# The end of a one-core block: h read back before the last two experts, their rows finished apart

## The chip, the cores and the metric

One core of a Trainium2 chip runs the whole program. The metric is device time in microseconds for one execution. All times inside an execution are given from the start of its span, the stretch from the first to the last instruction of the program that the profiler recorded. TensorE is called PE, VectorE DVE, ScalarE ACT, GpSimd POOL and SyncE SP.

## What is computed

One layer of a streaming encoder over 1024 tokens of 1024 channels, batch 1: a normalisation and one projection, two mixers (a diagonal state-space model and retention), an output projection that gives h, then a mixture of experts on top of h and a final normalisation. Only the last two matter here:

```python
    h = h + hier_moe(rms_norm(h, norm2_w), ...)
    return rms_norm(h, final_norm_w)

    # hier_moe: each token goes to 2 of 32 experts
    hid = jax.nn.silu(xb @ w_gate[e]) * (xb @ w_up[e])          # 1024 -> 512
    return ((hid @ w_down[e]) * w_b[:, None])                    # 512 -> 1024, added to the token's row
```

`rms_norm` multiplies a row by `rsqrt(mean(x*x) + eps)` and by a weight per channel.

## The kernel before

The sequence is cut into 8 tiles of 128 tokens (`NT = 8`). Mixers and output projection leave h in HBM as `h_d`, and the normalised rows as `hn_d`. A token may be routed to any expert; each expert takes up to 96 tokens (`CAP`), whose indices are a column of `tok` (padded with an index out of bounds) and whose weights are a column of `lacc[:, 1]`. An overflow loop at the very end takes further blocks of an expert that has more; here it runs no pass, but its barrier is executed.

The experts run one after the other, e = 0 to 31. For each, POOL gathers 96 rows of `hn_d` by index (`gather`, three experts ahead), PE transposes them (`x_split`), and every fp32 operand is split into a rounded part `hi` (a cast on ACT, L1241 for weights, L1221 for activations) and the rest `lo` (a subtraction on DVE, L1242 and L1222), so that a product is three matmuls: xh·hi, xh·lo, xl·hi. `in_proj` does gate ("g") and up ("u"), 24 matmuls each (L1267); ACT applies silu (L1378), DVE multiplies (L1387). The hidden rows wait one expert: in iteration e the order of the program is gate of e, then `hid_split` (transposes `ht`, L1275) and `down` of e − 1 (L1287), then up of e. `down` copies its two PSUM halves out with the weights (L1294, tile `yh` or `xy`) and POOL scatters them into `h_d` with an addition (`scatter`, L1210). Each scatter waits for the one before to land.

SP issues all loads of weights, at most six under way, in the order of the list `worder`. Its last four entries are pairs of tiles of h, read back from `h_d` (`wr_load`, L949, tiles `wh_0` to `wh_3`). They are issued once the number of experts scattered reaches `NE - 1`, and wait for the scatter of expert 30.

What follows the last expert: its rows are not scattered. They are gathered from `h_d` into `hg`, and the copy of its sums `y` is added there. Tiles 0 to 5 (`LATE = 6`) are finished without them; into tiles 6 and 7 they are added with a matmul by a selection matrix `late`, which POOL builds in `late_rows` (L1352, L1353). `final` finishes a tile: square with a row sum on ACT (L231), mean plus eps on DVE (L232), power −0.5 on POOL (L233), scaling by factor and channel weight on DVE (L1413); SP stores it (L1416). At the end POOL writes the finished rows `hg` over tiles 0 to 5 by index (L1450), after the stores of those six.

The instructions of each engine run in the order in which they were built. A scheduler makes that order from a simulated timeline; `behind(kind)` tells it to place what follows no earlier than the named instruction. Rows of that order name semaphores: DMAHW those of SP's transfers, DMASW those of POOL's.

Of the kernel before, what the change touches and what calls it, by code (L numbers as in the profile page):

```python
# [13 lines left out]
I32 = mybir.dt.int32  # L14
# [30 lines left out]
VF = 0  # L45
LATE = 6
NX = 3
# [100 lines left out]
def hybrid_block(ctx: ExitStack, tc: tile.TileContext, a: dict, out: bass.AP, dbg=None):  # L148
# [820 lines left out]
    def next_loads(n):  # L969

        while n > 0 and worder and (worder[0][1] != "h" or NDONE[0] >= NE - 1):
            wr_load(*worder.pop(0))
            n -= 1
        return n
# [283 lines left out]
    def in_proj(e, nm, xs):  # L1258
        pt = ps_g.tile([P, 512], F32, tag="g", name=f"{nm}{e}")
        n = 0  # L1260
        for half_ in range(2):
            for c, (hi, lo) in enumerate(take(e, nm, half_)):
                for q in range(2):
                    k = 4 * half_ + 2 * c + q
                    ws = slice(q * 512, q * 512 + 512)
                    for l, r in ((xs[0], hi), (xs[0], lo), (xs[1], hi)):
                        TE.matmul(pt[0:CAP], l[:, k, :], r[:, ws], start=(n == 0), stop=(n == 23))  # L1267
                        n += 1
        return pt
# [77 lines left out]

    def late_rows():

        n = (NT - LATE) * P  # L1350
        sel = late_at[0:CAP]
        G.iota(sel, pattern=[[1, n]], base=LATE * P - OOB, channel_multiplier=0, **small)  # L1352
        G.tensor_scalar(out=sel, in0=sel, scalar1=lacc[:, 0, NE - 1:NE], scalar2=None, op0=ALU.is_equal)  # L1353
        return sel

# [17 lines left out]
    for e in range(NE):  # L1373
# [27 lines left out]
        if e == NE - 2:  # L1401
            tabi, nbk, lasti = made
            late = late_rows()
        prev = (e, hid)


    def final(i, t, n=P):

        junk = yh[:, D + 512:2 * D].bitcast(BF)
        ss = pe.tile([P, 1], F32, tag="ss", bufs=4, name=f"fs{i}")  # L1410
        rr = pe.tile([P, 1], F32, tag="rr", bufs=4, name=f"fr{i}")
        rstd_of(t[0:n], D, ss[0:n], rr[0:n], junk[0:n])
        V.scalar_tensor_tensor(out=t[0:n], in0=t[0:n], scalar=rr[0:n, 0:1], in1=fw[0:n], op0=ALU.mult, op1=ALU.mult)  # L1413

# [4 lines left out]

    hs, last_tok = hid_split(*prev), tok[:, NE - 1:NE]  # L1420
    gather(hg, last_tok, h_d)
    pts = down_mm(NE - 1, hs)
    y = yh[:, 0:D]
    for q in range(2):
        qs = slice(q * 512, (q + 1) * 512)
        at["copy"] = S.activation(y[0:CAP, qs], pts[q][0:CAP], AF.Copy, scale=wts[:, NE - 1:NE])
# [10 lines left out]
    with behind("copy"), behind("split"):
        at["rows"] = V.tensor_tensor(out=hg[0:CAP], in0=hg[0:CAP], in1=y[0:CAP], op=ALU.add)
        for i in range(LATE, NT):
            for q in range(2):  # L1440
                qs = slice(q * 512, (q + 1) * 512)
                pt = (ps_g if q else ps_d).tile([P, 512], F32, tag="g" if q else "d", name=f"la{i}_{q}")
                TE.matmul(pt, late[:, (i - LATE) * P:(i - LATE + 1) * P], y[0:CAP, qs], start=True, stop=True)
                V.tensor_tensor(out=htile(i)[:, qs], in0=pt, in1=htile(i)[:, qs], op=ALU.add)
        for i in range(2, LATE):
            finish(i)
        final("g", hg, CAP)
        for i in range(LATE, NT):
            finish(i)
    rows = G.indirect_dma_start(out=out[0, 0:LATE * P, :], out_offset=bass.IndirectOffsetOnAxis(ap=last_tok, axis=0),  # L1450
                                in_=hg[0:CAP, :], in_offset=None, bounds_check=LATE * P - 1, oob_is_err=False)
    for d in stores[:LATE]:
        tc.add_manual_dep(rows.ins, d.name, SYNC, reason="these rows come after those stored without them")

# [89 lines left out]
```

## Time and profile before

| what | value |
|---|---|
| median of 3 runs | 1106.59 us (1105.11 to 1107.81) |
| the profiled execution, its own time | 1108.12 us |
| its span | 1106.4 us |
| PE busy (matmuls) | 1036.0 us, 94% |
| DVE busy | 851.7 us, 77% |
| ACT busy | 648.7 us, 59% |
| POOL busy | 315.2 us, 28% |
| HBM traffic over the span | 276 GB/s |

Busy time is a union of the instructions' own times. Matmuls are pipelined, so a busy PE is not one at its peak. The experts take the span from about 500 us on; the part that the change touches is the last 60 us. An idle time in brackets behind a row is that of the engine just before it, and the name behind the arrow is what ended it. Transfers show as their issue (SPq, or POOL's DMA_INDIRECT); the time to landing is counted from there.

### The profile page before, as it was taken

To read this page: it belongs to the slowest core of one execution; us is meant where nothing else is said; L and a number is where in the kernel's file an instruction comes from. 1 tells how busy PE (TensorE), PEld (TensorE's weight loads), DVE (VectorE), ACT (ScalarE), POOL (GpSimd) and SP (SyncE) were. 2 spreads that over 40 slices of the span, in tenths; PEclk is the share of its full clock that TensorE was granted. 3 is DMA by queue.
4 is the path that set the end of the run, shared out by engine and by line. 5 is a ranking of instruction groups with operands and counts; after the bars stand their busy time and mean duration, and the time that the engine had idled before them with its cause. 6 is when DMAs were issued, how large, how long until landed. Compare 5 with 4: busy or idle time off the path is not lost. (4 is left out here: it accounts for less than half of the span.)

```text
span 1106.4 us, 15386 instructions
## 1 busy us (share of the span) xinstructions
PE 1036.0 (94%) x5185; PEld 793.2 (72%) x5186; DVE 851.7 (77%) x1221; ACT 648.7 (59%) x867; POOL 315.2 (28%) x402
## 2 busy tenths in 40 slices
PE   6988889999999999988999999999999999999990
PEld 5776777888888888865777777777777777777750
DVE  4785898635446655567998999989898998999874
ACT  6512342243311222236888888888888888888862
POOL 4946477221046521122111010111101010231312
PEclk9988999999999899997999999999999999999995
DMA  8564465563524598867999999999999999999955
GB/s 307 214 190 101 89 190 130 147 207 114 181 77 153 197 341 275 286 267 258 358 362 384 365 380 374 363 352 353 371 349 373 359 360 356 387 359 365 384 172 209
DMA packets 88132, 305.88 MB, mean 276 GB/s; under 512 B 14588, under 2 KB 35324, under 8 KB 63472
## 3 DMA queue, kind: packets, MB, share of 16 engines
q1 hardware_dynamic: 80160, 287.38, 71.9%
q0 software_dynamic: 7280, 17.01, 6.4%
q8 instruction: 42, 0.69, 0.3%
q10 hardware_dynamic: 608, 0.46, 0.1%
q14 instruction: 42, 0.34, 0.1%
HBM read 266.05 MB, written 39.85 MB: 276 GB/s over the span
## 5 line engine op out<-in xcount | busy, mean ns | idle before, releaser
L1242 DVE TENSOR_TENSOR wlou<-wu,whiu 128x1024 fp32r<-128x1024 f32 x128 | 156.0, 1224 | 35.1 <-ACT whiu L1241 23.5
L1242 DVE TENSOR_TENSOR wlod<-wd,whid 128x1024 fp32r<-128x1024 f32 x128 | 153.8, 1216 | 3.4 <-PE dn L1287 1.2
L1242 DVE TENSOR_TENSOR wlog<-wg,whig 128x1024 fp32r<-128x1024 f32 x127 | 151.2, 1218 | 2.5 <-ACT whig L1241 0.2
L1241 ACT CAST whiu<-wu 128x1024 fp32r<-128x1024 f32 x128 | 134.2, 1048 | 25.3 <-PE dn L1287 16.7
L1241 ACT CAST whig<-wg 128x1024 fp32r<-128x1024 f32 x127 | 130.7, 1052 | 29.2 <-PE u L1267 28.3
L1241 ACT CAST whid<-wd 128x1024 fp32r<-128x1024 f32 x128 | 134.2, 1049 | 23.2 <-PE g L1267 14.2
L1267 PE MATMUL g<-wlog,xh 128*96 128x512 f32 x254 | 102.1, 402 | 0.0
L1267 PE MATMUL u<-whiu,xl 128*96 128x512 f32 x256 | 101.5, 396 | 0.0
L1267 PE MATMUL u<-whiu,xh 128*96 128x512 f32 x256 | 101.1, 395 | 0.0
L1267 PE MATMUL g<-whig,xh 128*96 128x512 f32 x254 | 100.8, 397 | 0.0
L1267 PE MATMUL g<-whig,xl 128*96 128x512 f32 x254 | 100.5, 396 | 0.0
L1267 PE MATMUL u<-wlou,xh 128*96 128x512 f32 x256 | 100.2, 391 | 0.0
L1287 PE MATMUL dn<-wlod,xh 128*96 128x512 f32 x256 | 99.6, 396 | 0.0
L1287 PE MATMUL dn<-whid,xl 128*96 128x512 f32 x256 | 96.1, 396 | 0.0
L1210 POOL DMA_INDIRECT h_d<-xy,tok x16 | 28.2, 1761 | 212.6 <-ACT xy L1294 196.7
L1287 PE MATMUL dn<-whid,xh 128*96 128x512 f32 x256 | 87.5, 395 | 0.6 <-ACT xh L1221 0.6
L1210 POOL DMA_INDIRECT h_d<-yh,tok x15 | 22.8, 1522 | 179.4 <-ACT yh L1294 163.3
L1287 PEld LDWEIGHTS dn<-whid,xh 128*96 128x96 f32 x256 | 41.6, 162 | 18.8 <-ACT xh L1221 0.8
L1267 PEld LDWEIGHTS u<-wlou,xh 128*96 128x96 f32 x256 | 41.4, 162 | 18.2
L1287 PEld LDWEIGHTS dn<-whid,xl 128*96 128x96 f32 x256 | 41.6, 163 | 17.8
L1267 PEld LDWEIGHTS u<-whiu,xl 128*96 128x96 f32 x256 | 41.1, 161 | 18.1
L1267 PEld LDWEIGHTS u<-whiu,xh 128*96 128x96 f32 x256 | 41.3, 161 | 17.8
(396 smaller groups left out, 2332.5 us busy)
## 6 DMA issues: line engine op xcount, KB each, us to landing
wg<-in_moe_w_gate_dram SPq DMA_DIRECT2D x64, 1024.0 KB
wu<-in_moe_w_up_dram SPq DMA_DIRECT2D x64, 1024.0 KB
wd<-in_moe_w_down_dram SPq DMA_DIRECT2D x64, 1024.0 KB
wr<-in_w_in_dram SPq DMA_DIRECT2D x19, 512.0 KB
xt<-in_x_dram SPq DMA_DIRECT2D x8, 512.0 KB
woraw<-in_w_out_dram SPq DMA_DIRECT2D x8, 512.0 KB
h<-in_x_dram SPq DMA_DIRECT2D x8, 512.0 KB
h_d<-h SPq DMA_DIRECT2D x8, 512.0 KB
```

Of the source, the lines that this page charges most:

```text
L1210: return G.indirect_dma_start(out=h_d, out_offset=bass.IndirectOffsetOnAxis(ap=idx, axis=0), in_=y[0:CAP, :], in_offset=None, bounds_check ...
L1241: S.copy(hi, raw)
L1242: at["split"] = V.tensor_tensor(out=lo, in0=raw, in1=hi.bitcast(F32), op=ALU.subtract)
L1267: TE.matmul(pt[0:CAP], l[:, k, :], r[:, ws], start=(n == 0), stop=(n == 23))
L1287: TE.matmul(pts[q][0:CAP], l[:, k, :], r[:, ws], start=(k == 0 and n == 0), stop=(k == 3 and n == 2))
```

## The change

`APART = 2` takes the place of `LATE = 6`. The four loads of h may be issued after 30 experts, and no longer see experts 30 and 31. All eight tiles are finished and stored without these two experts' rows. The rows of both are finished apart: expert 31's in `hg` as before, expert 30's gathered into `hg2` after its scatter. A token that both experts have would be written twice; `spread` and `only` compare the two lists (one small transpose on PE, four small DVE operations) and move such tokens out of bounds in `tokx`, the list for `hg2`. Two indexed writes end the program, each over all 1024 rows, after all eight stores.

The factors are made for two tiles at a time: `square` on ACT puts row sums (already divided by 1024, through the scale of the activation) into columns of `msqf`, `factors` adds eps (DVE, for the first pair POOL) and takes the power on POOL for two columns at once, `scaled` multiplies. The last expert's sums go from PSUM into `hg` with one DVE operation per half (weight and addition), squared per half. The selection matrix, its matmuls and `late_rows` are gone.

```diff
-LATE = 6
+APART = 2
-        while n > 0 and worder and (worder[0][1] != "h" or NDONE[0] >= NE - 1):
+        while n > 0 and worder and (worder[0][1] != "h" or NDONE[0] >= NE - APART):
...
-    def down_mm(e, hs):
+    def down_mm(e, hs, between=None):
         pts = [ps_d.tile([P, 512], F32, tag="d", name=f"dn{e}_{q}") for q in range(2)]
         for half_ in range(2):
-            for c, (hi, lo) in enumerate(take(e, "d", half_)):
+            with behind("square") if half_ else nullcontext():
+                pieces = take(e, "d", half_)
+            if between and not half_:
+                hs = between()
+            for c, (hi, lo) in enumerate(pieces):
...
-    def late_rows():
...
+    def spread():
+        V.tensor_copy(late_at[0:CAP, 0:CAP], lacc[:, 0, NE - 1:NE].to_broadcast([CAP, CAP]))
+
+    def only():
+        pt = ps_t.tile([P, 512], F32, tag="t", name="tx")
+        TE.matmul(pt[0:CAP, 0:CAP], late_at[0:CAP, 0:CAP], ident[0:CAP, 0:CAP], start=True, stop=True)
+        same, both = late_at[0:CAP, P:P + CAP], late_at[0:CAP, P + CAP:P + CAP + 1]
+        V.tensor_scalar(out=same, in0=pt[0:CAP, 0:CAP], scalar1=lacc[:, 0, NE - 2:NE - 1], scalar2=None, op0=ALU.is_equal)
+        V.tensor_reduce(out=both, in_=same, axis=AX.X, op=ALU.max)
+        V.tensor_scalar(out=both, in0=both, scalar1=float(OOB), scalar2=lacc[:, 0, NE - 2:NE - 1], op0=ALU.mult, op1=ALU.add)
+        V.tensor_scalar(out=tokx, in0=both, scalar1=float(OOB), scalar2=None, op0=ALU.add)
...
+        if e == NE - 1:
+            with behind("proj"), behind("cut"):
+                only()
         if prev is not None:
             hs = hid_split(*prev)
             down(prev[0], hs)
...
-            late = late_rows()
+            with behind("cut"):
+                spread()
...
+    def first_tiles():
+
+        with behind("whi"):
+            square(htile(0), 0)
+            square(htile(1), 1)
+        with behind("scatter"):
+            factors(0, 2, eng=G)
+        with behind("factors"):
+            gather(hg, last_tok, h_d)
+            at["factors"] = gather(hg2, tok[:, NE - 2:NE - 1], h_d)
+        with behind("split"):
+            finish(0)
+        with behind("square"):
+            hs = hid_split(*prev)
+        with behind("cut"):
+            finish(1)
+        return hs
+
+    pts = down_mm(NE - 1, None, first_tiles)
+    with behind("cast"):
+        square(htile(2), 2)
+        square(htile(3), 3)
+    with behind("square"), behind("split"), behind("factors"):
+        factors(2, 4)
+        for i in (2, 3):
             finish(i)
...
+        for i in range(4, NT):
+            square(htile(i), i)
+            if i % 2:
+                factors(i - 1, i + 1)
+                for j in (i - 1, i):
+                    finish(j)
+    with behind("square"), behind("factors"):
+        square(hg2[0:CAP], NT)
+        factors(NT, NT + 1, CAP)
+
+    with behind("split"):
+        for q in range(2):
+            qs = slice(q * 512, (q + 1) * 512)
+            V.scalar_tensor_tensor(out=hg[0:CAP, qs], in0=pts[q][0:CAP], scalar=wts[:, NE - 1:NE], in1=hg[0:CAP, qs],
+                                   op0=ALU.mult, op1=ALU.add)
+            square(hg[0:CAP, qs], NT + 1 + q)
...
+    scaled(hg2[0:CAP], fac[0:CAP, NT:NT + 1])
+    scaled(hg[0:CAP], fac[0:CAP, NT + 1:NT + 2])
+
+    def rows_out(t, idx):
+        rows = G.indirect_dma_start(out=out[0], out_offset=bass.IndirectOffsetOnAxis(ap=idx, axis=0),
+                                    in_=t[0:CAP, :], in_offset=None, bounds_check=T - 1, oob_is_err=False)
+        for d in stores:
+            tc.add_manual_dep(rows.ins, d.name, SYNC, reason="these rows come after those stored without them")
+
+    with behind("factors"):
+        rows_out(hg2, tokx[:, 0:1])
+        rows_out(hg, last_tok)
```

Three places show what the built order makes of this. The first is iteration 31, where the gate of expert 31 ends and the down product of expert 30 begins. On ACT `xh<-ht` is the cast of expert 30's transposed hidden rows, `yh<-g` is silu, `whid` and `whiu` are the rounded parts of down and up weights. Before:

```order
L1241 CAST whid_01_9825<-wd_0_9363 128x1024
L1221 CAST xh<-ht_9812 128x384
L1241 CAST whid_10_9841<-wd_1_9391 128x1024
L1378 ACTIVATE yh<-g_9770 96x512
L1241 CAST whid_11_9845<-wd_1_9391 128x1024
L1241 CAST whiu_00_9867<-wu_0_9413 128x1024
```

In the change:

```order
L1241 CAST whid_01_9839<-wd_0_9364 128x1024
L1241 CAST whid_10_9855<-wd_1_9392 128x1024
L1388 ACTIVATE yh<-g_9778 96x512
L1241 CAST whid_11_9859<-wd_1_9392 128x1024
L1221 CAST xh<-ht_9826 128x384
L1241 CAST whiu_00_9881<-wu_0_9414 128x1024
```

On PE, in the same place, the transposes `ht` and the gate's last products; before:

```order
L1267 MATMUL g_9770<-whig_01_9775,xl 96x512
L1267 MATMUL g_9770<-whig_10_9791,xh 96x512
L1275 MATMUL ht_9812<-cst_g,yh 128x96 x4
L1267 MATMUL g_9770<-wlog_10_9792,xh 96x512
L1267 MATMUL g_9770<-whig_10_9791,xl 96x512
L1267 MATMUL g_9770<-whig_10_9791,xh 96x512
```

In the change (`tx` is the small transpose of `only`):

```order
L1267 MATMUL g_9778<-wlog_11_9804,xh 96x512
L1267 MATMUL g_9778<-whig_11_9803,xl 96x512
L1359 MATMUL tx<-cst_g,ovf 96x96
L1275 MATMUL ht_9826<-cst_g,yh 128x96 x4
L1291 MATMUL dn_0_9833<-whid_00_9835,xh 96x512
L1291 MATMUL dn_0_9833<-wlod_00_9836,xh 96x512
```

The transposes moved from inside the gate product behind its end, and their cast moved behind silu and behind the second half of the down weights.

The second place is POOL's queue from the scatters of experts 27 to 30 on (`h_d<-yh`, `h_d<-xy`). Before:

```order
L1352 IOTA ovf 96x256 [waits DVE_49,PE_49]
L1353 TENSOR_SCALAR ovf<-ovf,lacc 96x256 [waits Pool_49]
L1210 DMA h_d<-yh,tok 1024x1024 [waits DMASW1_49,Activation_49]
L1210 DMA h_d<-xy,tok 1024x1024 [waits DMASW3_49,Activation_49]
L1210 DMA h_d<-yh,tok 1024x1024 [waits DMASW4_49,Activation_49]
L1210 DMA h_d<-xy,tok 1024x1024 [waits DMASW6_49,DMASW5_49,Activation_49]
L1205 DMA fwh<-h_d,tok 96x1024 [waits DMASW6_49]
L233 TENSOR_TENSOR fr_9971<-fs_9970,half_c 128x1 [waits DVE_49]
```

In the change, from the scatter of expert 28 to the end:

```order
L1210 DMA h_d<-xy,tok 1024x1024 [waits DMASW3_49,Activation_49]
L1210 DMA h_d<-yh,tok 1024x1024 [waits DMASW4_49,Activation_49]
L1210 DMA h_d<-xy,tok 1024x1024 [waits DMAHW5_49,DMAHW0_49,DMAHW6_49,DMASW6_49,DMAHW7_49,DMASW5_49,Activation_49]
L1442 TENSOR_SCALAR msqf<-msqf 128x2 [waits Activation_49]
L1443 TENSOR_TENSOR msqf<-msqf,half_c 128x2 [waits Pool_49]
L1205 DMA fwh<-h_d,tok 96x1024 [waits DMASW6_49]
L1205 DMA ovf<-h_d,tok 96x1024 [waits DMASW0_49,DVE_49]
L1443 TENSOR_TENSOR msqf<-msqf,half_c 128x2 [waits DVE_49] x3
L1443 TENSOR_TENSOR msqf<-msqf,half_c 96x1 [waits DVE_49]
L1503 TENSOR_TENSOR msqf<-msqf,half_c 96x1 [waits DVE_49]
L1508 DMA out_dram<-ovf,tokx 1024x1024 [waits DMAHW4_49,DMAHW3_49,DMAHW5_49,DMAHW2_49,DMAHW6_49,DMAHW1_49,DMAHW7_49,DMAHW0_49,DVE_49]
L1508 DMA out_dram<-fwh,tok 1024x1024 [waits DMASW2_49,DMASW1_49,DVE_49]
```

Before, POOL's queue ended so:

```order
L233 TENSOR_TENSOR fr_10019<-fs_10018,half_c 128x1 [waits DVE_49,Pool_49]
L233 TENSOR_TENSOR frg<-fsg,half_c 96x1 [waits DVE_49,Pool_49]
L233 TENSOR_TENSOR fr_10032<-fs_10031,half_c 128x1 [waits DVE_49,Pool_49]
L233 TENSOR_TENSOR fr_10039<-fs_10038,half_c 128x1 [waits DVE_49,Pool_49]
L1450 DMA out_dram<-fwh,tok 768x1024 [waits DMAHW4_49,DMAHW3_49,DMAHW5_49,DMAHW2_49,DMAHW6_49,DMAHW1_49,DMASW0_49]
```

The two selections left the head of the scatters; the scatter of expert 30 now names four DMAHW semaphores, those of the loads of h; gathers stand between the factors of the first pair and those of the second; the one indexed write behind six stores became two, the first behind eight, the second with two DMASW semaphores.

The third place is the tail on ACT and DVE behind the last up product. ACT before:

```order
L1241 CAST whid_01_9932<-wd_0_9481 128x1024
L1241 CAST whid_10_9948<-wd_1_9513 128x1024
L1241 CAST whid_11_9952<-wd_1_9513 128x1024
L1221 CAST xh<-ht_9916 128x384
L231 ACTIVATE yh,fs_9970<-wh_0_9875 128x1024
L231 ACTIVATE yh,fs_9977<-wh_0_9875 128x1024
L1426 ACTIVATE yh<-dn_0_9926,lacc 96x512
L1426 ACTIVATE yh<-dn_1_9927,lacc 96x512
L231 ACTIVATE yh,fs_9997<-wh_1_9877 128x1024
```

In the change:

```order
L1241 CAST whid_01_9929<-wd_0_9482 128x1024
L1439 ACTIVATE yh,msqf<-wh_0_9722 128x1024 x2
L1221 CAST xh<-ht_9945 128x384
L1241 CAST whid_10_9966<-wd_1_9514 128x1024
L1241 CAST whid_11_9970<-wd_1_9514 128x1024
L1439 ACTIVATE yh,msqf<-wh_1_9724 128x1024 x2
L1439 ACTIVATE yh,msqf<-wh_2_9726 128x1024 x2
L1439 ACTIVATE yh,msqf<-wh_3_9728 128x1024 x2
L1439 ACTIVATE yh,msqf<-ovf 96x1024
```

DVE before (`wlod` the down weights' rest, `yh<-u` the hidden product, `wh` tiles of h):

```order
L1242 TENSOR_TENSOR wlod_00_9929<-wd_0_9481,whid_00_9928 128x1024
L1242 TENSOR_TENSOR wlod_01_9933<-wd_0_9481,whid_01_9932 128x1024
L1242 TENSOR_TENSOR wlod_10_9949<-wd_1_9513,whid_10_9948 128x1024
L1387 TENSOR_TENSOR yh<-u_9866,yh 96x512
L1222 TENSOR_TENSOR xl<-ht_9916,xh 128x384
L1242 TENSOR_TENSOR wlod_11_9953<-wd_1_9513,whid_11_9952 128x1024
L232 TENSOR_SCALAR fs_9970<-fs_9970 128x1
L232 TENSOR_SCALAR fs_9977<-fs_9977 128x1
L1413 SCALAR_TENSOR_TENSOR wh_0_9875<-wh_0_9875,fr_9971,fwh 128x1024
```

In the change:

```order
L1242 TENSOR_TENSOR wlod_00_9926<-wd_0_9482,whid_00_9925 128x1024
L1242 TENSOR_TENSOR wlod_01_9930<-wd_0_9482,whid_01_9929 128x1024
L1400 TENSOR_TENSOR yh<-u_9880,yh 96x512
L1222 TENSOR_TENSOR xl<-ht_9945,xh 128x384
L1242 TENSOR_TENSOR wlod_10_9967<-wd_1_9514,whid_10_9966 128x1024
L1242 TENSOR_TENSOR wlod_11_9971<-wd_1_9514,whid_11_9970 128x1024
L1442 TENSOR_SCALAR msqf<-msqf 128x2
L1430 SCALAR_TENSOR_TENSOR wh_0_9722<-wh_0_9722,msqf,fwh 128x1024 x2
L1442 TENSOR_SCALAR msqf<-msqf 128x2
L1430 SCALAR_TENSOR_TENSOR wh_1_9724<-wh_1_9724,msqf,fwh 128x1024 x2
L1442 TENSOR_SCALAR msqf<-msqf 128x2
L1430 SCALAR_TENSOR_TENSOR wh_2_9726<-wh_2_9726,msqf,fwh 128x1024 x2
```

On ACT two squares moved ahead of the last hidden cast and all the others follow each other behind the weights; on DVE the third piece of the down weights moved behind the hidden product, and the scalings follow each other in pairs.

## Rows read from the trace of the kernel before

**Rows 1.** The page's span; queue instructions of L1540 (count, ns min/median/max, starts)

```profile
span 1106.4 us, 15386 instructions
...
L1540 POOLq DRAIN  x3: 46/108/5385, 1100.1 to 1106.1; - x3
```

**Rows 2.** Timeline of POOL: start us, us, line, what, [idle before <-releaser]

```profile
1022.73 0.35 POOL L1352 IOTA ovf<- 96x256 f32 x1 [22.59 <-PE tbm L1338]
...
1024.49 1.78 POOL L1210 DMA_INDIRECT h_d<-yh,tok  x1 [0.18 <-issue]
...
1047.74 1.86 POOL L1210 DMA_INDIRECT h_d<-yh,tok  x1 [9.12 <-DMA h_d<-xy,tok]
1062.42 1.42 POOL L1210 DMA_INDIRECT h_d<-xy,tok  x1 [12.82 <-ACT xy L1294]
1068.57 1.03 POOL L1205 DMA_INDIRECT fwh<-h_d,tok  x1 [4.73 <-DMA h_d<-xy,tok]
...
1076.12 1.53 POOL L233 TENSOR_TENSOR fr<-fs,half_c 128x1 f32<-128x1 f32 x1 [0.60 <-DVE fs L232]
...
1094.64 0.98 POOL L1450 DMA_INDIRECT out_dram<-fwh,tok  x1 [1.99 <-DMA out_dram<-wh]
```

**Rows 3.** DMA issues of 1066 to 1107; last number: us to landing

```profile
fwh<-h_d,tok POOLq DMA_INDIRECT x1, 8.1
out_dram<-fwh,tok POOLq DMA_INDIRECT x1, 4.7
```

**Rows 4.** SP's stores to the output in 1090 to 1092

```profile
L1416 SPq DMA_DIRECT2D out_dram<-wh x1: 332/332/332, 1090.5 to 1090.5; - x1
```

**Rows 5.** Timeline of DVE, the last 40 us

```profile
1067.67 0.68 DVE L1387 TENSOR_TENSOR yh<-u,yh 96x512 f32<-96x512 f32 x1
...
1082.97 1.29 DVE L1444 TENSOR_TENSOR wh<-la,wh 128x512 f32<-128x512 f32 x2 [2.81 <-DMA wh<-h_d]
...
1092.18 2.48 DVE L1413 SCALAR_TENSOR_TENSOR wh<-wh,fr,fwh 128x1024 f32<-128x1024 f32 x2 [0.38 <-POOL fr L233]
```

**Rows 6.** Waits of SP's queue, 1030 to 1107: us, times, longest

```profile
SPq L949 <- DMA h_d<-xy,tok: 22.3, 1, 22.3
```

**Rows 7.** Timeline of SP's queue

```profile
1068.36 2.25 SPq L949 DMA_DIRECT2D wh<-h_d  x4
```

**Rows 8.** Timeline of ACT

```profile
1008.36 1.26 ACT L1294 ACTIVATE yh<-dn,lacc 96x512 f32<-96x512 f32 x2
...
1043.73 1.25 ACT L1294 ACTIVATE yh<-dn,lacc 96x512 f32<-96x512 f32 x2
...
1055.58 0.59 ACT L1378 ACTIVATE yh<-g 96x512 f32<-96x512 f32 x1 [0.34 <-PE g L1267]
1056.07 1.04 ACT L1241 CAST whid<-wd 128x1024 fp32r<-128x1024 f32 x1
...
1068.99 0.48 ACT L1221 CAST xh<-ht 128x384 fp32r<-128x384 f32 x1 [1.25 <-PE ht L1275]
1073.51 1.06 ACT L231 ACTIVATE yh<-wh 128x1024 bf16<-128x1024 f32 x1 [4.05 <-DMA wh<-h_d]
...
1074.70 1.06 ACT L231 ACTIVATE yh<-wh 128x1024 bf16<-128x1024 f32 x1
```

**Rows 9.** Timeline of PE, expert 31

```profile
1052.49 0.49 PE L1275 MATMUL ht<-cst_g,yh 96*128 96x96 f32 x4
...
1055.15 0.39 PE L1267 MATMUL g<-whig,xl 128*96 128x512 f32 x1
1055.38 0.62 PE L1287 MATMUL dn<-whid,xh 128*96 128x512 f32 x2
...
1066.26 0.40 PE L1267 MATMUL u<-whiu,xl 128*96 128x512 f32 x1
```

**Rows 10.** The four scatters from 1000 on (L1210)

```profile
DMA to landing us min/median/max: 5.9/9.5/12.4
```

**Rows 11.** Windows: us, busy us of each engine, PEclk, DMA share, GB/s

```profile
1069.90:1073.30 3.40, 3.40 (x10) 2.20 (x9) 1.38 (x2) 0.00 (x0) 0.00 (x0) 0.50 0.94 367
```

More of the change, by code (lines that the diff above doesn't have):

```diff
@@ L1240, in w_split @@
         hi, lo = pair or [pe.tile([P, 1024], F32R, tag="w" + c, bufs=NHL[c], name=f"w{c}{nm}") for c in ("hi", "lo")]
-        S.copy(hi, raw)
+        at["whi"] = S.copy(hi, raw)
         at["split"] = V.tensor_tensor(out=lo, in0=raw, in1=hi.bitcast(F32), op=ALU.subtract)
@@ L1266, in in_proj @@
                     for l, r in ((xs[0], hi), (xs[0], lo), (xs[1], hi)):
-                        TE.matmul(pt[0:CAP], l[:, k, :], r[:, ws], start=(n == 0), stop=(n == 23))
+                        at["proj"] = TE.matmul(pt[0:CAP], l[:, k, :], r[:, ws], start=(n == 0), stop=(n == 23))
                         n += 1
@@ L1346, in tables @@
         yield tabi, nbk, lasti
-    def late_rows():
[L1350 to L1354, printed above, removed]
+    tokx = pl_.tile([CAP, 1], I32, name="tokx")
+    def spread():
[8 more added lines that the diff above has]
+        V.tensor_scalar(out=tokx, in0=both, scalar1=float(OOB), scalar2=None, op0=ALU.add)
     first = [gather(xg[e], tok[:, e:e + 1]).ins for e in range(NX)]
@@ L1392, in hybrid_block @@
             fw, hg = fwh[:, 0:D], fwh[:, D:2 * D]
-            late_at = ovf[:, 2048 - (NT - LATE) * P:2048]
+            late_at = ovf[:, 2048 - 2 * P:2048]
             nc.sync.dma_start(fw, a['final_norm_w'].to_broadcast([P, D]))
@@ L1409, in final, with scaled, square, factors @@
         junk = yh[:, D + 512:2 * D].bitcast(BF)
-        ss = pe.tile([P, 1], F32, tag="ss", bufs=4, name=f"fs{i}")
-        rr = pe.tile([P, 1], F32, tag="rr", bufs=4, name=f"fr{i}")
+        ss = pe.tile([P, 1], F32, tag="ss", bufs=2, name=f"fs{i}")
+        rr = pe.tile([P, 1], F32, tag="rr", bufs=2, name=f"fr{i}")
         rstd_of(t[0:n], D, ss[0:n], rr[0:n], junk[0:n])
-        V.scalar_tensor_tensor(out=t[0:n], in0=t[0:n], scalar=rr[0:n, 0:1], in1=fw[0:n], op0=ALU.mult, op1=ALU.mult)
+        scaled(t[0:n], rr[0:n, 0:1])
+    def scaled(t, r):
+        at["scaled"] = V.scalar_tensor_tensor(out=t, in0=t, scalar=r, in1=fw[0:t.shape[0]], op0=ALU.mult, op1=ALU.mult)
+    msqf = pe.tile([P, 2, NT + 3], F32, name="msqf")
+    msq, fac = msqf[:, 0], msqf[:, 1]
+    def square(t, j):
+        n, f = t.shape
+        junk = yh[:, D + 512:D + 512 + f // 2].bitcast(BF)
+        at["square"] = S.activation(junk[0:n], t, AF.Square, scale=1.0 / math.sqrt(D), accum_out=msq[0:n, j:j + 1])
+    def factors(j0, j1, n=P, eng=V):
+        eng.tensor_scalar(out=msq[0:n, j0:j1], in0=msq[0:n, j0:j1], scalar1=EPS, scalar2=None, op0=ALU.add)
+        at["factors"] = G.tensor_tensor(out=fac[0:n, j0:j1], in0=msq[0:n, j0:j1],
+                                        in1=half_c[0:n, 0:1].to_broadcast([n, j1 - j0]), op=ALU.pow)
     def store(i, t):
         return nc.sync.dma_start(out[0, i * P:(i + 1) * P, :], t).ins
[L1420 to L1426, printed above, removed]
+    last_tok, hg2 = tok[:, NE - 1:NE], ovf[:, 0:D]
     htile = lambda i: wq[(NE, "h", i // 2)][:, (i % 2) * 1024:(i % 2) * 1024 + 1024]
@@ L1430, in finish @@
     def finish(i):
-        final(i, htile(i))
+        scaled(htile(i), fac[:, i:i + 1])
         stores.append(store(i, htile(i)))
-    with behind("cast"), behind("split"):
-        for i in range(2):
-            finish(i)
[L1437 to L1453, printed above, removed]
+    def first_tiles():
[14 more added lines that the diff above has]
+        return hs
@@ new lines, in hybrid_block @@
+    with behind("split"):
[4 more added lines that the diff above has]
+            square(hg[0:CAP, qs], NT + 1 + q)
+    last_sq = msq[0:CAP, NT + 1:NT + 2]
+    V.scalar_tensor_tensor(out=last_sq, in0=last_sq, scalar=EPS, in1=msq[0:CAP, NT + 2:NT + 3], op0=ALU.add, op1=ALU.add)
+    at["factors"] = G.tensor_tensor(out=fac[0:CAP, NT + 1:NT + 2], in0=last_sq, in1=half_c[0:CAP, 0:1], op=ALU.pow)
```

## The prediction, on record before the result

> **What bounds the kernel now.** I read the trace from its end. The span closes at 1106.4 us. The last long entry is a drain of POOL of 5.4 us that begins at 1100.1, in the barrier around the overflow loop, which runs no pass here [rows 1]. Ahead of that barrier stands one transfer: the indexed write of the last expert's rows (L1450). POOL starts it at 1094.64 [rows 2] and it lands 4.7 us later [rows 3], at 1099.3. So the span ends 7.1 us after the last indexed write has landed, and this distance is the same in both programs.
>
> What starts that write? Its row says that POOL stood idle until a store of `out_dram` landed [rows 2]. It is the store of tile 5, which SP issued at 1090.5 [rows 4], so 4.1 us pass from the store that matters to the start of the write. The stores follow DVE, which scales the last pair of tiles from 1092.18 to 1094.66 [rows 5]. Why is DVE that late? The reading of h waited: SP stood 22.3 us for the scatter of expert 30 [rows 6] and issued the four loads from 1068.36 on [rows 7]. ACT's first square waited 4.05 us for the first of them, until 1073.51 [rows 8], and DVE 2.81 us for the last, until 1082.97 [rows 5]. The tail is one string: scatter 30, h, squares, scaling, stores, indexed write, barrier. Ahead of it PE sets the pace, one matmul of 512 columns each 0.23 us without a hole [rows 9].
>
> **The change, part by part.**
>
> 1. *h is read two experts early.* The loads now wait for scatter 29. In this trace POOL started it at 1047.74 [rows 2]; the last four scatters took 5.9 to 12.4 us to land, median 9.5 [rows 10], so about 1057.3. It will come sooner: the two instructions that selected the late rows (L1352, L1353) are gone from POOL's queue. The first stood there waiting for PE until 1022.73, so that scatter 27 went at 1024.49 [rows 2], though its copy on ACT was done by 1009.6 [rows 8]; scatter 29 in turn sat 9.12 us until scatter 28 had landed [rows 2], though its copy ended at 1045.0 [rows 8]. With the chain unblocked I let 29 start at 1045.3 and land at 1054.8. The four loads then run alone. Before, the first landed 5.1 us after its issue and the last 14.6 us after it [rows 5, 7, 8], beside a gather and two stores. Alone I estimate 12.6, so the last of h is there at 1067.4; at worst, with 1057.3 and 14.6, at 1071.9.
>
> 2. *What stands behind it on POOL.* Scatter 30 now waits for all four loads (the DMAHW names in its row). It starts at 1067.6 and, with the queues idle, takes the 5.9 us of [rows 10]: 1073.5. Behind it in POOL's queue stand the factors of tiles 0 and 1, which need no landing, then two gathers that need scatter 30, then the factors of tiles 2 and 3. Two gathers of 1.03 us [rows 2] and their start end at 1075.9; a power took up to 1.53 us on POOL [rows 2], so 1077.4. DVE wants those factors at 1077.7 (below). The cover is 0.3 us, and past it every microsecond counts in full. The first gather, started at 1073.8, lands at 1081.9 if it takes the 8.1 us of [rows 3] again; DVE adds its rows after tile 5, at 1082.7.
>
> 3. *A hole on PE in expert 31.* `only()` is placed behind the gate's last matmul, and the built order has expert 30's transposes (`ht`) there too; they stood inside the gate product before. On ACT their cast `xh<-ht` now follows silu and the cast of `whid_11`. Before, the last gate matmul started at 1055.15 and the first down matmul at 1055.38; the transposes inside cost 0.28 [rows 9]. Now the gate ends 0.28 sooner, silu starts 0.43 later as before, so at 1055.30, the next cast 0.49 behind it and lasts 1.04 [rows 8], the cast of ht takes 0.48 more: PE resumes at about 1057.3. The hole is 1.9 us. The few small DVE operations of `spread` and `only` lie inside it.
> What reaches the tail is less. Before, the product of up and silu (L1387) started 1.41 us after the last up matmul began, at 1066.26 [rows 5, 9], because DVE was still splitting three pieces of the down weights; now the third stands behind it. I take 0.5 us in place of 1.4, so 1.0 of the 1.9 stays; the bounds are 0 and 1.9. The last hidden cast moves from 1068.99 [rows 8] to 1070.0. The squares of tiles 0 and 1, now ahead of it on ACT, have their h since 1060 and fit into ACT's idle time there.
>
> 4. *The tail on ACT and DVE.* From 1070.0: cast 0.5, two casts of weights 1.0 each, two squares (2 and 3) 1.2 each, as the two squares of [rows 8] stand apart: 1074.9. On DVE the step "add eps" for tiles 2 and 3 stands ahead of the scaling of tile 0, so DVE starts at 1075.1. It scales eight tiles at 1.24 each (2.48 for a pair [rows 5]), 9.9 us, with two sums of 96 rows between (1.3 us, as the pair at L1444 [rows 5]) and 0.3 for small steps: 1086.6, against 1094.66 before. This is the gain, 8.1 us. The products with the selection matrix, their four additions and the copy of the last expert's sums are gone; DVE's share of that is in the difference.
>
> 5. *Two lists in place of one, one behind the other.* Before, the write waited for six stores, and the last two landed beside it. Now the first list waits for all eight, and the second for the landing of the first (its row in POOL's order names two software queues). So 4.1 us from the last store to the first list: 1090.7. Its price: 4.7 measured with two stores beside it [rows 3]; without them less, but not below the 0.98 of issue [rows 2] plus the transfer. I take 4.6 for each: 1095.3, 0.2 to start the second, 1100.1. Before, 1099.3. The scaling of the two sets of rows (2.5 us on DVE behind 1086.6) is hidden behind the last store's landing.
> The sum has 9.2 us for the two lists. The Trainium skill ("DMA: Bandwidth & Descriptors", section "Anatomy of one DMA — SWDGE (gpsimd) path") has about 2.0 us fixed plus bytes at 436 GB/s, mostly spent on confirming the write; by it 0.39 MB would be an estimated 2.9 us, 3.9 with the issue measured here, and the sum 1.4 us lower. It also speaks against the change: that fixed cost is now paid twice in a row.
>
> **The sum.** 1100.1 plus 7.1 is 1107.2 in the span, 0.8 above 1106.4. DVE's last scaling of a tile comes 8.1 sooner, but the way from there to the end of the span grows from 11.7 to 20.6 us: it now waits for the last store, not the sixth, and for a second list. The profiled execution took 1108.12, 1.7 over its span and 1.5 over the median of 1106.59; it would be 1108.9. For the median I forecast 1106.59 + 0.8 = 1107.4.
>
> **The rivals.**
> *Slower, POOL's queue:* scatter 29 lands at 1057.3 as before and the loads take 14.6 as before. Scatter 30 starts at 1071.9 and lands at 1077.8, the gathers are out at 1080.2, the factors at 1081, 3.4 us after DVE wants them: 1110.8. It decides from a landing of scatter 30 later than 1073.8. For it: landings from 5.9 to 12.4, and a cover of 0.3. Against it: from 1068 on nothing else moves, and scatter 30 had its 5.9 in such a quiet. A smaller share of it would be seen within the forecast.
> *Slower, the clock:* after the idle at 1066.7 the granted clock stood at 0.50 for the 3.4 us from 1069.9 [rows 11]; PE did ten matmuls in place of some fifteen. If the new hole does the same, PE loses another 1.5: 1108.9, at the edge of what can be told.
> *Faster, cheap lists:* the lists and the last store run with nothing beside them, 4.0 for each list and 0.8 off the 4.1 (estimates: the rows show both with company), and DVE takes up the whole hole (1.0): 1107.4 − 1.2 − 0.8 − 1.0 = 1104.4. For it: the bound of 0 in step 3. Against it: three terms must all come out low.
> *Faster, the change does not do what its order says:* the second list does not stay for the first, and 4.8 us go: 1102.6.
>
> **How the numbers follow.** Forecast 0.57; POOL's queue 0.20; clock 0.08; cheap lists 0.10; no second wait 0.05. About 0.2%, 2.2 us, is what a measurement here tells from no change, so "same" is 1104.4 to 1108.8. Slower: POOL's queue, half of the clock and a little of the forecast's own upper end, 0.27. Faster: no second wait, most of the cheap lists, 0.13. Same: 0.60. The range takes in the forecast, the clock and most of POOL's queue, and below it the cheap lists: 1104.2 to 1110.2.
>
> **What the profile of the changed kernel would show.** The loads of h issued near 1055 (right) or 1057 and later (the slower rival). A hole on PE near 1055 with `xh<-ht` on ACT behind it. Scatter 30 issued when the last h lands, near 1067.6. DVE's scalings from 1075 to 1086.6 without a wait for POOL. Two indexed writes, the second started just after the first landed, and 7.1 us from the last landing to the end. I am wrong if DVE's last scaling ends much off 1086.6, or if the time from it to the end is not some 20.6 us.

## The result, and the profile after

The changed kernel takes 1113.13 us (median of 20 runs, 1109.32 to 1116.73); the kernel before took 1107.53 in the same sessions. The ratio is 1.0051, with a 95% interval of 1.0039 to 1.0063: about 5.6 us slower. I had forecast 1107.4, and a range that ended at 1110.2.

Its profiled execution took 1116.12 us, with a span of 1114.4. Part of the distance to the 1106.4 of before [rows 1] lies ahead of anything that the change touches. One and the same matmul of the first expert, in PE's timeline of before:

```profile
514.38 0.39 PE L1267 MATMUL u<-whiu,xl 128*96 128x512 f32 x1
```

and of after:

```profile
518.54 0.40 PE L1267 MATMUL u<-whiu,xl 128*96 128x512 f32 x1
```

A window ahead of it (us, busy us of PE, weight loads, DVE, ACT and POOL with their counts, granted clock, DMA share, GB/s), before:

```profile
350.00:394.00 44.00, 41.09 (x270) 35.88 (x269) 29.94 (x51) 12.03 (x17) 28.95 (x33) 0.92 0.62 209
```

and after:

```profile
350.00:394.00 44.00, 40.23 (x250) 36.03 (x249) 29.27 (x50) 10.87 (x15) 27.79 (x26) 0.84 0.54 183
```

Up to that matmul the same code took 4.2 us longer; in this window of it the mean granted clock of TensorE was 0.84 in place of 0.92. So I count every profile from that matmul to the end of its span, and call that length its tail. Both kernels were profiled twice more for that (below, h1 and h2):

| kernel | ratio to before, interval | first expert at | span | tail: from there to the end |
|---|---|---|---|---|
| before | 1 | 514.4; 511.7; 514.4 | 1106.4; 1102.8; 1105.6 | 592.0; 591.1; 591.2 |
| after | 1.0051 (1.0039 to 1.0063) | 518.5; 512.0; 513.4 | 1114.4; 1106.5; 1109.1 | 595.9; 594.5; 595.7 |
| e1, lists side by side | 1.0008 (0.9992 to 1.0024) | 515.3 | 1110.0 | 594.7 |
| e2, a weight load less | 1.0014 (1.0001 to 1.0027) | 517.4 | 1111.4 | 594.0 |
| e3, scatter 30 elsewhere | 0.9995 (0.9981 to 1.0009) | 514.5 | 1106.1 | 591.6 |
| e4, no hole on PE | 1.0057 (1.0041 to 1.0073) | 518.1 | 1112.6 | 594.5 |
| g1, gathers last | 1.0050 (1.0032 to 1.0069) | 516.1 | 1116.4 | 600.3 |
| f1, neither wait | 0.9986 (0.9971 to 1.0000) | 515.6 | 1106.2 | 590.7 |
| f3, f1 with a new tail | 0.9958 (0.9942 to 0.9974) | 514.2 | 1102.7 | 588.5 |

From the first expert on the change costs 3.9 us (mean 595.37 against 591.43). Up to the copy of expert 29's sums the two run level: it starts at 1047.83, in the kernel before at 1043.73 [rows 8], 4.1 us apart as the first expert is. What follows is the end of the span, in the times of the profile shown; to set them beside the prediction's, take 4.2 off.

The loads of h are issued behind scatter 29, as planned. The timeline of SP's queue:

```profile
1046.88 2.82 SPq L952 DMA_DIRECT2D wd<-in_moe_w_down_dram  x2
1058.31 3.13 SPq L949 DMA_DIRECT2D wh<-h_d  x4
```

and its waits (us, times, longest):

```profile
SPq L949 <- DMA h_d<-yh,tok: 8.6, 1, 8.6
```

1058.3 is 1054.1 on the clock of the prediction, which had 1054.8. The wait is 8.6 in place of 22.3 [rows 6]. But the loads don't run alone. Windows from their issue on:

```profile
1058.30:1062.00 3.70, 2.21 (x14) 1.60 (x13) 3.02 (x5) 2.61 (x4) 0.00 (x0) 1.00 0.81 298
1062.00:1066.00 4.00, 4.00 (x19) 2.75 (x18) 3.16 (x5) 2.38 (x3) 0.00 (x0) 1.00 1.02 420
1066.00:1070.00 4.00, 4.00 (x19) 2.81 (x18) 3.12 (x3) 3.92 (x6) 0.00 (x0) 1.00 1.03 411
1070.00:1074.00 4.00, 3.18 (x16) 1.91 (x14) 3.08 (x4) 1.56 (x2) 0.00 (x0) 1.00 0.28 105
1074.00:1077.20 3.20, 1.06 (x3) 0.74 (x4) 0.69 (x2) 3.17 (x7) 0.00 (x0) 0.89 0.05 17
```

The next-to-last column is the reading: all sixteen DMA engines are busy from 1062 to 1070 (0.81 of them before that), then a few, and from 1074 to 1077.2 a share of 0.05, less than one engine of sixteen. The trace's landing records say the same of the fourth load: eleven of its sixteen parts land by 1070.95, two near 1071.9, two near 1074.5, the last at 1077.11. The last part of expert 31's last weight load had landed only at 1066.03, 7.7 us after the first load of h was issued. From there the last parts of the four loads follow at 1068.58, 1071.11, 1073.63 and 1077.11.

The records don't name the DMA engine, but the distance from the last part of the weights to the last part of h is nearly the same in all seven profiles in which scatter 30 waits for h: 11.1 us in the three of the changed kernel, in e1 and in e2, 11.0 in g1, 10.8 in e4. What differs is how late the weights end, 5.5 to 8.8 us after the first load of h was issued, and with it the whole reading of h takes 16.3 to 19.9. Before, where the weights had ended 5.8 to 7.2 us ahead of the first load of h, all sixteen parts of a load landed within 1.4 us of each other.

What stands behind the last part is POOL. Its queue's waits ahead of scatter 30, by line (ns min, median, max; first and last start):

```profile
L1210 POOLq EVENT_SEMAPHORE  x3: 43/43/8527, 1068.6 to 1077.3; - x3
```

and its timeline, with the copy on ACT that scatter 30 takes:

```profile
1066.68 1.25 ACT L1298 ACTIVATE xy<-dn,lacc 96x512 f32<-96x512 f32 x2
...
1078.02 1.57 POOL L1210 DMA_INDIRECT h_d<-xy,tok  x1 [27.24 <-ACT whid L1241]
...
1079.98 0.74 POOL L1443 TENSOR_TENSOR msqf<-msqf,half_c 128x2 f32<-128x2 f32 x1
1083.91 1.09 POOL L1205 DMA_INDIRECT fwh<-h_d,tok  x1 [3.19 <-DMA h_d<-xy,tok]
1085.31 0.99 POOL L1205 DMA_INDIRECT ovf<-h_d,tok  x1 [0.30 <-issue]
1086.33 1.39 POOL L1443 TENSOR_TENSOR msqf<-msqf,half_c 128x2 f32<-128x2 f32 x2
...
1099.32 0.97 POOL L1508 DMA_INDIRECT out_dram<-ovf,tokx  x1 [2.38 <-SPq L1521]
1103.37 0.92 POOL L1508 DMA_INDIRECT out_dram<-fwh,tok  x1 [3.08 <-issue]
```

Scatter 30 had its copy at 1068 and went at 1078.0. (The releaser named in its bracket, ACT, had long been done; the semaphore row above shows the true wait.) The gathers stayed for its landing, the factors of tiles 2 to 5 for the gathers, and DVE for the factors. DVE's timeline:

```profile
1080.76 2.48 DVE L1430 SCALAR_TENSOR_TENSOR wh<-wh,msqf,fwh 128x1024 f32<-128x1024 f32 x2 [0.35 <-POOL msqf L1443]
...
1087.08 2.48 DVE L1430 SCALAR_TENSOR_TENSOR wh<-wh,msqf,fwh 128x1024 f32<-128x1024 f32 x2 [3.76 <-POOL msqf L1443]
...
1093.26 2.47 DVE L1430 SCALAR_TENSOR_TENSOR wh<-wh,msqf,fwh 128x1024 f32<-128x1024 f32 x2
```

The tiles end at 1095.73, which is 1091.6 by the clock of before: 3.1 us sooner than there [rows 5], not 8.1. Then come the two lists in a row, and the barrier (POOL's drain, ns and first start, as in [rows 1]):

```profile
L1602 POOLq DRAIN  x3: 46/108/5548, 1108.0 to 1114.1; - x3
```

### The profile page after: what moved, and what is told of

Its sections match the earlier page's. It is cut to its first block, busy times and chain, and to the rows that moved or that the text cites. A ratio compares the mean times of both kernels' runs of the same rounds, so it can differ in the third digit from the quotient of the medians.

```text
span 1114.4 us, 15369 instructions
## 1 busy us (share of the span) xinstructions
PE 1036.3 (93%) x5179; PEld 796.1 (71%) x5180; DVE 851.4 (76%) x1220; ACT 648.8 (58%) x869; POOL 309.1 (28%) x400
## 5 line engine op out<-in xcount | busy, mean ns | idle before, releaser
L1210 POOL DMA_INDIRECT h_d<-xy,tok x16 | 25.9, 1617 | 234.9 <-ACT xy L1298 200.1
L1210 POOL DMA_INDIRECT h_d<-yh,tok x15 | 22.2, 1477 | 196.0 <-ACT yh L1298 189.0
## 6 DMA issues: line engine op xcount, KB each, us to landing
wr<-in_w_in_dram SPq DMA_DIRECT2D x19, 512.0 KB, 7.5
xt<-in_x_dram SPq DMA_DIRECT2D x8, 512.0 KB, 6.5
woraw<-in_w_out_dram SPq DMA_DIRECT2D x8, 512.0 KB
h<-in_x_dram SPq DMA_DIRECT2D x8, 512.0 KB
h_d<-h SPq DMA_DIRECT2D x8, 512.0 KB, 4.3
```

The lines of the kernel that those rows point to most:

```text
L1210: return G.indirect_dma_start(out=h_d, out_offset=bass.IndirectOffsetOnAxis(ap=idx, axis=0), in_=y[0:CAP, :], in_offset=None, bounds_check ...
```

## The experiments

All edits are to the changed kernel unless said. Lengths "to the end" are those of the table.

**e1, the lists side by side.**

```
+        return rows.ins
...
-        rows_out(hg2, tokx[:, 0:1])
-        rows_out(hg, last_tok)
+        apart = rows_out(hg2, tokx[:, 0:1])
+        tc.declare_no_dep(rows_out(hg, last_tok), apart, reason="no row stands in both lists")
...
```

> The second list no longer stays for the landing of the first (no row stands in both). Theory (the two lists in a row cost their full price): the second starts about 1.0 us after the first, as soon as POOL has issued it, in place of 4.05, so 3.0 to 3.5 us go from the end: the time stands at 1.0020 to 1.0025 of before in place of 1.0051, some 2.3 us above it. Rival (the software queue moves one list after the other anyway): the second still lands 3.5 us behind the first, and the time stays at 1.005.

POOL's timeline:

```profile
1097.00 0.97 POOL L1508 DMA_INDIRECT out_dram<-ovf,tokx  x1 [2.38 <-SPq L1522]
1098.28 0.93 POOL L1508 DMA_INDIRECT out_dram<-fwh,tok  x1 [0.30 <-POOLq L1522]
```

and the lists' time to landing (last number, us):

```profile
out_dram<-ovf,tokx POOLq DMA_INDIRECT x1, 3.1
out_dram<-fwh,tok POOLq DMA_INDIRECT x1, 4.4
```

The second list starts 1.28 us behind the first in place of 4.05, and takes 4.4 in place of some 3.6 beside it. From the first list to the end of the span it is 13.0 us, against 15.1: 2.1 us. The tail of the table is only 0.7 shorter, since in this execution the way to the first list was longer than in the changed kernel (581.7 us from the first expert, against 579.6 to 580.8). The runs give 4.7, from two ratios that are each uncertain by more than 1 us. I had expected 3.0 to 3.5: the profile shows less and the runs more. So the second list's place in a row costs 2 us by the profile, up to 4.7 by the runs, and the rival, which had the time stay at 1.005, falls.

**e2, one weight load less.**

```
-    worder += [(NE - 1, "d", 0), (NE - 1, "d", 1)]
+    worder += [(NE - 1, "d", 0)]
...
-        t = wq[(e, nm, half_)]
+        t = wq[(e, nm, 0 if (e, nm) == (NE - 1, "d") else half_)]
```

> The last of expert 31's eight weight loads (1 MB of the down weights) is left out and its first half is used twice, so the output of that expert is not the reference's. Theory (the reading of h stands behind the weights on the DMA queues): the last of h lands about 2.5 us sooner, scatter 30 and the factors behind it too, and the time falls by 2 to 3 us, to about 1.0028 of before. Rival (the four loads of h need their 18.8 us whatever is ahead of them, or the tail is set elsewhere): under 0.5 us, so 1.005.

The runs fell by 4.1 us and the tail by 1.4, one above and one below the 2 to 3 expected. The last part of h lands 556.7 us after the first expert; in the three profiles of the changed kernel at 558.6, 556.8 and 557.9. That is 1.1 sooner than their mean, the right way, but within their scatter, and the built order changed beside it (DVE scales tiles 0 and 1 ahead of the last piece of weights). So the time of this run doesn't test the theory: the weights' own last part came only 1.1 us sooner (545.6 after the first expert, against 547.5, 545.7 and 546.8), and not the 2.5 that the edit was meant to take away. What speaks for the queue of weights is the landing records: h follows them by 11.1 us here too.

**e3, scatter 30 elsewhere.**

```
-        at["scatter"] = scatter(y, tok[:, e:e + 1])
+        at["scatter"] = scatter(y, tok[:, e:e + 1], hn_d if e == NE - 2 else h_d)
```

> Scatter 30 goes to another DRAM tensor, so it waits for no load of h, and the rows gathered lack expert 30 (the output of some rows is not the reference's). Theory (POOL's queue behind the wait for h sets the tail): scatter 30 starts some 10 us sooner, right behind its copy, DVE's 3.8 us of waiting for the factors go, and so does the late start of the scaling; 3.5 to 4.5 us go, to 1.0010 to 1.0020 of before. Rival (the hole on PE or the two lists make the loss): under 1 us, 1.0045 or more.

```profile
1064.21 1.42 POOL L1210 DMA_INDIRECT hn_d<-xy,tok  x1 [17.43 <-ACT xy L1298]
...
1078.70 4.87 DVE L1430 SCALAR_TENSOR_TENSOR wh<-wh,msqf,fwh 128x1024 f32<-128x1024 f32 x4
```

The scatter goes as soon as its copy is there, DVE's 3.8 us of waiting for POOL is gone (0.2 is left, and 0.9 for ACT), and the tail is 591.6: 3.8 less, as expected. The runs give 6.3, more than expected. That is as much as the whole loss against the kernel before (591.4, and 0.9995). And h itself came no sooner: its last part landed 561.0 us after the first expert, later than in any profile of the changed kernel (556.8 to 558.6). So what costs the time is not h's arrival at the tiles but what it holds up in POOL's queue. The edit frees two waits there at once, scatter 30's for h and the gathers' for scatter 30, and the built order on DVE changed beside it (tiles 0 and 1 ahead of the last two pieces of weights); how much each is worth it doesn't tell.

**e4, no hole on PE.** `only()` stands behind `hid_split`, without the order "behind the last gate matmul".

> only() and expert 30's transposes stand inside the gate product again, as before the change. Theory (the tail waits for h, so the hole is covered): PE's 1.5 us idle ahead of the down product of expert 30 goes, and the end moves by 0 to 0.5 us: 1.0047 to 1.0051. Rival (the hole is what the change lost): 1.6 to 2 us go, 1.0034 or less.

In the changed kernel PE stood idle in expert 31 for 1.49 us:

```profile
1061.29 0.47 PE L1291 MATMUL dn<-whid,xh 128*96 128x512 f32 x1 [1.49 <-ACT xh L1221]
```

In e4 the down product follows the gate product at once:

```profile
1059.01 0.40 PE L1267 MATMUL g<-whig,xl 128*96 128x512 f32 x1
1059.24 0.62 PE L1291 MATMUL dn<-whid,xh 128*96 128x512 f32 x2
```

Nothing comes of it: 1.0057 against 1.0051, and a tail of 594.5, the lower end of the changed kernel's own. The hole is covered by the wait for h, as expected.

**g1, the gathers last.** The two gathers move behind the factors of all tiles; scatter 30 waits as before.

> Only POOL's order is changed: the two gathers, which stay for the landing of scatter 30, stand behind the factors of all eight tiles and not ahead of those of tiles 2 to 7. Scatter 30 still waits for the four loads of h. Theory (what DVE waits for is POOL's queue, blocked by the landing that the gathers need): DVE's 3.8 us of waiting go, the gathers leave later but have the last stores to hide behind; 2 to 4 us go, to 1.0015 to 1.0033 of before. Rival (scatter 30's own late start is what counts, the gathers are nothing): under 1 us, 1.0042 or more.

The ratio did not move, and the profile says why. The timeline of DVE, ACT and POOL:

```profile
1085.20 4.87 DVE L1430 SCALAR_TENSOR_TENSOR wh<-wh,msqf,fwh 128x1024 f32<-128x1024 f32 x4 [0.74 <-POOL msqf L1443]
...
1096.02 1.06 ACT L1439 ACTIVATE yh<-ovf 96x1024 bf16<-96x1024 f32 x1 [13.53 <-DMA ovf<-h_d,tok]
...
1100.62 1.59 POOL L1508 DMA_INDIRECT out_dram<-ovf,tokx  x1 [0.58 <-issue]
```

and the gathers' time to landing:

```profile
fwh<-h_d,tok POOLq DMA_INDIRECT x1, 6.5
ovf<-h_d,tok POOLq DMA_INDIRECT x1, 8.2
```

The tiles are done 574.0 us after the first expert, 3.2 sooner than in the changed kernel: the gathers' place did hold up DVE. But now the gathers run beside the stores, take 6.5 and 8.2 us (4.4 and some 4.6 before), and the rows become late: the first list starts at 1100.62, 10.6 us after the last scaling, in place of 3.6. The expectation had the wait right and its cover wrong. The tail of 600.3 is from the slowest of the six runs (1118.11, their median 1115.54), so it shows the order of things better than their price. With scatter 30 waiting for h, moving the gathers in POOL's queue only chose which of two things was late; what helped was to free scatter 30 (e3).

**h1 and h2, both kernels again.**

> The kernel before, profiled again. The two profiles so far differ by 4.2 us ahead of the first expert, in code that the change leaves alone. If that part is chance, its length scatters here too (514 to 519 us to the first matmul u<-whiu,xl), while the length from there to the end stays at 592.0 within 0.7 us. If it belongs to the change, both profiles of this kernel begin the experts near 514.4.

> The changed kernel, profiled again. If the part ahead of the experts is chance, it scatters between 514 and 519 us, and from there to the end it takes 595.9 within 1 us (3.9 us more than before); if the medians' 5.6 us lie in the tail, it takes 597 or more.

> As h1_before, a third profile of the kernel before: from the first expert to the end 592.0 within 0.7 us.

> As h1_after, a third profile of the changed kernel: from the first expert to the end 595.9 within 1 us, or 597 and more if the tail holds the medians' 5.6 us.

The start of the first expert scatters in both kernels (511.7 to 514.4, and 512.0 to 518.5, wider than expected), so one profile of each can't tell them apart there. The tails are 591.1 to 592.0 and 594.5 to 595.9; three of the four new ones lie up to 0.4 us below the bounds that I had set, and the two ranges stay 2.5 us apart. In the changed kernel the tail follows the last part of h: 594.5, 595.7 and 595.9 us, with h at 556.8, 557.9 and 558.6. The tail holds 3.9 of the medians' 5.6 us, whose interval begins at 4.3. Where the rest lies stays open: scatter ahead of the experts would be enough for it, but was not counted over the 20 runs. Tail and ratio differ elsewhere too (e1 gained 0.7 by the one and 4.7 by the other); e3 is the experiment in which both give back the whole loss.

**f1 and f3, towards a better version.** f1 does without scatter 30, and starts the second list beside the first, as e1. Both sets of rows are gathered behind scatter 29; expert 30's sums are added on DVE to its own rows, and to expert 31's by a product with the 0/1 matrix that `only` makes anyway. Its core:

```
-        at["scatter"] = scatter(y, tok[:, e:e + 1])
+        if e < NE - 2:
+            at["scatter"] = scatter(y, tok[:, e:e + 1])
...
+            with behind("scatter"):
+                gather(hg, tok[:, NE - 1:NE], h_d)
+                gather(hg2, tok[:, NE - 2:NE - 1], h_d)
...
+                V.tensor_tensor(out=hg2[0:CAP], in0=xy[0:CAP, D:2 * D], in1=hg2[0:CAP], op=ALU.add)
...
+                    TE.matmul(pts[q][0:CAP], late_at[0:CAP, P:P + CAP], xy[0:CAP, D + q * 512:D + q * 512 + 512], start=True, stop=False)
```

> A version with the reference's output that takes both waits away: scatter 30 is gone (both sets of rows are gathered behind scatter 29; expert 30's sums are added to theirs on DVE, and to expert 31's rows by a product with the 0/1 matrix of only() in the same PSUM, with the weight of expert 31 moved into its hidden values), and the second list does not stay for the first. Theory (two separate losses in one string): the 4.7 us of the lists and the 6.3 us of the scatter add up to some 10 us: 0.995 to 0.997 of before. Rival (one covers the other): no better than the scatter alone, 0.999.

> f1 with the hole on PE gone, the squares of tiles 0 and 1 written elsewhere so that they need not stay for the last product of up and silu, 'add eps' on POOL, and DVE's tail in one order: expert 31's transposed hidden values, the last two pieces of weights, the eight tiles without a pause, then the rows. Theory (with the waits for POOL gone DVE's own work sets the tail, so what starts it earlier counts in full): another 2 to 4 us off f1, 0.992 to 0.995 of before. Rival (h's landing or the squares on ACT set it): as f1 within 1 us.

f1 is 0.9986, tail 590.7. That is what its rival said, no better than the scatter alone. The first list starts 2.0 us later than in e3 (counted from the first expert): 1.4 of it are there at the last scaling, DVE now having an addition of 1.22 us that the scatter did, and 0.6 come behind it. All additions stand ahead of the last pair of tiles, as in e3. f3 puts those of expert 31 behind it and that of expert 30 ahead of the tiles, and starts earlier; the timeline of POOL and DVE:

```profile
1070.18 0.24 POOL L1456 TENSOR_SCALAR msqf<-msqf 128x2 f32<-128x2 f32 x1 [11.00 <-ACT yh L1453]
1070.50 0.74 POOL L1457 TENSOR_TENSOR msqf<-msqf,half_c 128x2 f32<-128x2 f32 x1
...
1073.70 2.47 DVE L1444 SCALAR_TENSOR_TENSOR wh<-wh,msqf,fwh 128x1024 f32<-128x1024 f32 x2
1076.79 2.48 DVE L1444 SCALAR_TENSOR_TENSOR wh<-wh,msqf,fwh 128x1024 f32<-128x1024 f32 x2 [0.61 <-POOL msqf L1457]
...
1079.92 1.31 POOL L1456 TENSOR_SCALAR msqf<-msqf 128x2 f32<-128x2 f32 x1
1081.32 1.60 POOL L1457 TENSOR_TENSOR msqf<-msqf,half_c 128x2 f32<-128x2 f32 x1
...
1089.48 1.59 POOL L1515 DMA_INDIRECT out_dram<-ovf,tokx  x1 [0.63 <-SPq L1529]
1091.38 0.93 POOL L1515 DMA_INDIRECT out_dram<-fwh,tok  x1 [0.30 <-POOLq L1529]
```

The scaling begins 2.7 us sooner than in the changed kernel, and the first list 5.5, both counted from the first expert. At 1104.57 us (median of 6; ratio 0.9958, 0.9942 to 0.9974) f3 beats both kernels. It is some 3 us better than f1, as forecast, but short of the 0.992 to 0.995 that I had set. It changes several things at once, and what each is worth was not measured.

## Why the prediction was wrong, point by point

**Step 1 is the one that failed.** "The four loads then run alone" had the issue right (1054.8 forecast, 1054.1 measured on that clock) and the company wrong. The loads took 18.8 us from the first issue to the last part, in place of 12.6, since expert 31's weights were still coming, and the last of sixteen parts of each load came behind theirs, by the landing records above. My 12.6 us for the loads holds for most of each load: eleven of the fourth one's sixteen parts were there 552.4 us after the first expert, where the forecast had 553.0. A load is there with its last part, and that came 558.6 after: 5.5 us late. The profile of before could have told it. At the very time for which I planned the loads, the DMA engines were not idle:

```profile
1050.00:1054.20 4.20, 4.20 (x22) 3.00 (x21) 4.19 (x5) 3.45 (x5) 0.00 (x0) 1.00 0.77 258
1054.20:1058.00 3.80, 3.80 (x18) 2.66 (x17) 3.50 (x4) 3.46 (x4) 0.00 (x0) 1.00 0.35 120
1058.00:1062.00 4.00, 4.00 (x19) 2.80 (x18) 3.55 (x4) 3.27 (x5) 0.00 (x0) 1.00 0.10 41
```

A share of 0.10 for the last 4 us is one or two engines of sixteen, and the last part of the last weight load landed at 1062.61 there, 7.8 us after 1054.8. I had read the loads' company where they stood in the kernel before, not where they were to go.

**Step 2** followed from it. The mechanism, its order and the place were right: with a cover of 0.3 us and h 5.5 us late, the factors of tiles 2 and 3 let DVE go on at 1087.08, or 1082.9 on the clock of before, 5.2 us after the 1077.7 at which I had DVE want them. DVE was late itself and waited 3.76 of that. Scatter 30's own 5.6 us to landing and the gathers' 1.0 each were as priced.

**Step 3** was nearly right and of no weight: the hole was 1.49 (1.9 forecast), the product of up and silu 0.8 late (1.0), and none of it reached the end (e4).

**Step 4** had an error of its own. The squares of tiles 0 and 1 don't fit into ACT's idle time there: they write to the scratch from which that product still reads, so ACT stood 2.44 us for DVE and the last hidden cast came 1.5 us later than forecast (1075.63, 1071.5 on the clock of before). Rows of DVE's and ACT's timelines:

```profile
1072.67 0.69 DVE L1400 TENSOR_TENSOR yh<-u,yh 96x512 f32<-96x512 f32 x1 [0.28 <-PE u L1267]
1073.39 1.06 ACT L1439 ACTIVATE yh<-wh 128x1024 bf16<-128x1024 f32 x1 [2.44 <-DVE yh L1400]
...
1075.63 0.46 ACT L1221 CAST xh<-ht 128x384 fp32r<-128x384 f32 x1
```

The scaling so began at 1076.6, not 1075.1. By the rows above this cost nothing by itself in the changed kernel: POOL's factors for tiles 2 and 3 waited for the gathers, not for DVE, so without it DVE would have waited for them some 5 us in place of 3.76 (an estimate; no run takes the scratch alone). f3 moves the scratch. The durations were right (2.48 for a pair of tiles).

**Step 5** was too dear: the lists were 3.3 and some 3.6 us to landing in place of 4.6, and the last store, issued at 1095.76, led to the first list in 3.56 in place of 4.1. Against that, the second list started 0.8 after the first had landed, not 0.2, and from the second landing to the end it took 7.4, not 7.1. From the last scaling to the end it took 18.7, not 20.6. The page of the Trainium skill that I had weighed there ("DMA: Bandwidth & Descriptors", section "Anatomy of one DMA — SWDGE (gpsimd) path") was the nearer of the two: 3.9 with the issue, against 3.3 and 3.6 measured. Its fixed cost is one per transfer, and that two lists in a row pay it twice fits e1: side by side the pair took 5.7 us from the first start to the second landing, in a row 7.6.

**The sum** by these: 5.0 later at the last scaling, all of it from h's late last part by way of POOL's queue, and 1.9 less behind it: 3.1 above the forecast, or 1110.3 for the span on the clock of before. That is the rival "POOL's queue" by mechanism and, at 1110.6 to 1110.8, nearly by price. The price came out partly by luck: scatter 29 landed on time, the loads took longer than even the rival had, and the cheaper lists gave some back. I gave it 0.20 and ended the range below it, though its condition, a landing of scatter 30 later than 1073.8 (it landed at 1079.4 on that clock), needed only one of the two things that I had taken at their best. The median moved by 1.7 us more than the tail, and that part none of the steps explains. The clock rival fell: the granted clock stays at 1.00 through the hole (the windows above). The second list does wait, and the cheap lists came but were outweighed.

## What to carry to other kernels

Before a transfer is moved earlier, read the DMA share at the place where it goes, down to shares of a tenth: a transfer is there with its last part, here 6.2 us after the eleventh of sixteen. Ask too which writer must then wait for it as a reader, and what is queued behind that writer: here the read of h moved ahead of a scatter, and the scatter took POOL's whole queue with it. Taking the writer off that queue (e3) gained more than the other order tried around it (g1).

## What was not expected of the hardware

One transfer's sixteen parts landed over 6.6 us (1070.46 to 1077.11), and how late the last one came went with the last part of the weights issued ahead of it. POOL's small steps grew while DVE scaled tiles: the addition of eps on 128x2 elements took 0.24 us alone and 1.31 beside it, the power 0.74 and 1.60 (f3), so DVE, relieved of that addition in f3, waited 0.6 us for POOL at each pair of tiles but the first. Two indexed writes side by side took 3.1 and 4.4 us, 3.3 and 3.6 in a row. The same instructions ahead of the experts took 511.7 to 518.5 us, with a mean granted clock of 0.84 to 1.00 between 350 and 394 us; these 6.8 us are more than the whole effect of this change.
